# Loading b_re and b_im in their own order and turning them on TensorE, in a hybrid state space and attention layer

## The chip, the cores and the metric

The kernel runs on one core of a Trainium2 chip. The metric is the device time of one execution in microseconds (us), lower is better. A core has five engines with instruction queues of their own: TensorE (PE, matmuls and transposes, with PEld for its weight loads), VectorE (DVE), ScalarE (ACT), GpSimd (POOL) and SyncE (SP, which here only issues transfers). ACT can issue transfers too; in the profile such issues stand as ACTq, those of SP as SPq. Every engine works through its own queue in order, and semaphores order the engines among each other.

## The reference

One decoder layer on x of 512 tokens by 1024 channels, in float32. The part that the change touches is the state space branch: 64 groups of 16 channels, each with 64 complex states. From lambda, dt and B it makes a discrete system:

```
dt = exp(log_dt)[:, None]
ab = exp(lam_re * dt) * (cos(lam_im * dt) + i sin(lam_im * dt))     # [group, state]
f  = (ab - 1) / (lam_re + i lam_im)
bb_re = f_re[..., None] * b_re - f_im[..., None] * b_im              # [group, state, channel]
bb_im = f_re[..., None] * b_im + f_im[..., None] * b_re
```

u, a slice of `rms_norm(x) @ w_in`, is driven through `h[t] = ab * h[t-1] + bb u[t]`; the real part of C h plus a skip goes through GELU and a gated projection. The other branch is dilated attention with three head groups. Both are gated, added, projected and added to x. `b_re` and `b_im` have the shape (64 groups, 64 states, 16 channels): 256 KB each, 4 KB per group, and 64 bytes for one group and state.

## The kernel before, in words

All large matmuls are done three times on two-part operands (a rounded high part and a rest, `mm3`, L105 to L108). Weights come in tiles of 1024 x 128 or 512 x 256 through `load_w` (L160): a load into `w_raw` (two buffers) from the SP queue (L164), a high part on ACT (L91) and a rest on DVE, or for the first two tiles on POOL (L93), into `w_hi` and `w_lo` (three buffers). A raw buffer is free again when both parts have been made from it.

The start: four blocks of x are loaded (L191), with the first two weight tiles between them. For each half of x, ACT squares and sums (L206), DVE makes the reciprocal root (L98 to L103), ACT and DVE scale (L212, L214), PE transposes 16 blocks (L221) into four banks of PSUM, and ACT and DVE write the high part and the rest of hT from them (L225, L226). Then PE makes the first three tiles of u for each half (L282 to L287).

The coefficients: `lr`, `li` and `dt` (lambda and the log of dt) are loaded from the SP queue (L293 to L295). DVE works out exp, sine, cosine, f and the first eight powers `pw` of ab as [group, state] (L298 to L373). PE turns them to [state, group] (L383, L389), and ACT copies them to `AT` and `fT` (L385, L391). Positions (L477) and the weights of the head norms (L511, L513) are loaded from the SP queue too; DVE makes angles and tables from them.

B: `dd` is one tile with four parts of [128, 64 groups, 16 channels]: D1, D2, BB and BB2. D1 holds b_re in its lower 64 partitions (one per state) and b_im in the upper ones; D2 holds -b_im and b_re. Each of the four halves is a load from the SP queue through a view [state, group, channel] (L406 to L409), in runs of 16 floats, 64 bytes; POOL changes the sign of one half of D2 (L410). BB and BB2 are D1 and D2 times fT (L417 to L422, on POOL and DVE). They go into the coefficients `ab` of eight groups at a time (L248 to L250), which PE transposes (L267) for the states' inputs (L278); a scan over 64 chunks on DVE follows (L584, L588). Later D1 and D2 are used again as buffers for other matrices (L653). PSUM: `bank` (L83) hands out the four buffers with the tag "g", used by the transposes of x, by `atp`, `ftp` and by most steps after.

The order: the program is written in the order above, but the four loads of b stand behind the first tiles of u and the powers. A scheduler (L1030, `schedule_with_timeline_sim=True`) takes the instructions as a simulated timeline finds them ready, and writes the order of each engine's queue from that. So in the trace the loads of b are issued right behind those of x and lambda, well ahead of the place where the code has them. The orders of all queues are fixed before the run; a real wait then holds everything behind it on that queue.

Of the kernel before, what the change touches and what calls it, by code (L numbers as in the profile page):

```python
# [11 lines left out]
F32 = mybir.dt.float32  # L12
F32R = mybir.dt.float32r
I32 = mybir.dt.int32
AF = mybir.ActivationFunctionType
ALU = mybir.AluOpType
# [4 lines left out]
P = 128  # L21
# [3 lines left out]
NB = S // P  # L25
G = 64
N = 64
Q = 16
T = 8
C = S // T  # L30
# [20 lines left out]
def tile_hybrid_block(ctx: ExitStack, tc: tile.TileContext, x, positions, norm_w, w_in, lam_re, lam_im,  # L51
                      log_dt, b_re, b_im, c_re, c_im, d_skip, w_glu, q_norm_w, k_norm_w, w_ssm_out,
                      w_attn_out, w_o, out, dbg=None):
    nc = tc.nc
    pe, act, dve, pool, sp = nc.tensor, nc.scalar, nc.vector, nc.gpsimd, nc.sync
    dbg = dbg or {}

    cst = ctx.enter_context(tc.tile_pool(name="cst", bufs=1))
# [24 lines left out]
    def bank(name):  # L83
        return ps_g.tile([P, 512], F32, name=name, tag="g")
# [26 lines left out]
    n_ra = 2                          # residual gates of the attention branch done early  # L111
# [92 lines left out]
    for h in range(2):  # L204
# [10 lines left out]
        for q in range(KT // 2):  # L215
            ps = bank("hps")
# [23 lines left out]
    def coef(dst, j, a1, a2, n0, n1, t, eng):  # L240
        """dst[p, g, i, :] = re(A^(8-i)) a1 + im(A^(8-i)) a2, i in n0..n1, for the j-th run of groups"""
        n, ng = n1 - n0, dst.shape[1]
        sh = [P, ng, n, Q]
        gs = slice(ng * j, ng * j + ng)
        ar = AT[:, 0, gs, n0:n1].unsqueeze(3).broadcast_to(sh)
        ai = AT[:, 1, gs, n0:n1].unsqueeze(3).broadcast_to(sh)
        tv = t[:, 0:ng * n * Q].rearrange("p (g k q) -> p g k q", g=ng, k=n)
        dve.tensor_tensor(dst, a1.unsqueeze(2).broadcast_to(sh), ar, op=ALU.mult)  # L248
        eng.tensor_tensor(tv, a2.unsqueeze(2).broadcast_to(sh), ai, op=ALU.mult)  # L249
        dve.tensor_tensor(dst, dst, tv, op=ALU.add)  # L250
# [42 lines left out]
    sp.dma_start(lr, lam_re[0])  # L293
    sp.dma_start(li, lam_im[0])
    sp.dma_start(dt, log_dt.rearrange("o g -> g o"))  # L295

# [45 lines left out]
    # pw[:, 0/1, tau-1, :] powers 1..8 of the discrete diagonal; pw index 8 holds f  # L342
# [21 lines left out]
    for n in (1, 2, 4):  # L364
        # powers n+1..2n = (1..n) * n
        br_ = pw[:, 0:1, n - 1:n, :].broadcast_to([G, 2, n, N])
        bi_ = pw[:, 1:2, n - 1:n, :].broadcast_to([G, 2, n, N])
        a = pw[:, :, 0:n, :]
        o = pw[:, :, n:2 * n, :]
        dve.tensor_tensor(o, a, br_, op=ALU.mult)  # L370
        dve.tensor_tensor(tq[:, :, 0:n], a, bi_, op=ALU.mult)
        dve.tensor_tensor(o[:, 0], o[:, 0], tq[:, 1, 0:n], op=ALU.subtract)
        dve.tensor_tensor(o[:, 1], o[:, 1], tq[:, 0, 0:n], op=ALU.add)  # L373
    # to [state (twice), group]
    AT = cst.tile([P, 2, G, 9], F32, name="AT")         # powers 8 to 0
# [16 lines left out]
    # step of the chunk recurrence, [(parity, state), out, in, pair]  # L392
# [9 lines left out]
    # B: [re; im] and its rotation by i  # L402
    dd = big.tile([P, 4, G, Q], F32, name="dd", tag="s1")
    D1, D2, BB, BB2 = (dd[:, i] for i in range(4))
    bv = [b_re[0].rearrange("g n q -> n g q"), b_im[0].rearrange("g n q -> n g q")]
    sp.dma_start(D1[0:64], bv[0])  # L406
    sp.dma_start(D1[64:128], bv[1])
    sp.dma_start(D2[0:64], bv[1])
    sp.dma_start(D2[64:128], bv[0])  # L409
    pool.tensor_scalar(D2[0:64], D2[0:64], -1.0, None, op0=ALU.mult)  # L410
# [34 lines left out]
    def silu2(dst, ps):  # L445
        """2 silu"""
        th = t2k("th")
        act.activation(th, ps, AF.Tanh, scale=0.5)
        dve.scalar_tensor_tensor(dst, th, 1.0, ps, op0=ALU.add, op1=ALU.mult)  # L449
# [25 lines left out]
    # rope angles  # L475
# [33 lines left out]
    # weights of the head norms; q carries -1/8  # L509
# [17 lines left out]
    # tables: tC = [c w1, c w2], tS = [-s w2, s w1], per group, q/k, residue  # L527
# [12 lines left out]
    def tok_granule():  # L540
        """[token, 256] of two residues per bank"""
# [66 lines left out]
    gT_hi = big.tile([P, KT, S], F32R, name="gT_hi", tag="s3")  # L608
    gT_lo = big.tile([P, KT, S], F32R, name="gT_lo", tag="s4")
    kd = dram.tile([8, Q, 8, 240], F32, name="kd")      # lags 7..0, then 7 lags of zeros  # L610
# [4 lines left out]
    def ca_unit(j):  # L615
        """C A^k of groups 8j..8j+7"""
# [17 lines left out]
        # skip weights on the diagonal  # L634
# [5 lines left out]
    def m_unit(j, ca, dg):  # L640
        """the block Toeplitz matrices of groups 8j..8j+7"""
# [28 lines left out]
    def y_unit(j, ca, M, Uj, Ss):  # L670
        ysb = t2k("ysb").rearrange("c (t m) -> c t m", t=4)
        ps = bank("yps")
        for g in range(8):
            # the later half of a chunk comes first in M and ca, and goes to the upper partitions
# [9 lines left out]
    def g_unit(j, ysb):  # L684
# [3 lines left out]
        # [r h c] -> [r c h], then gelu  # L688
# [42 lines left out]
    def qk_granule(hp, g, QT, KA, KB):  # L731
# [16 lines left out]
        # rotary part of every head  # L748
# [30 lines left out]
    def scores(hp, QT, KA, KB):  # L779
        Pt = big.tile([P, 2, 2, NB, 256], F32, name="Pt", tag="s3")  # L780
        st = sml.tile([P, 2, 2, 2, NB], F32, name="st")      # kind (A, B), stat (-max, sum), head, block
# [33 lines left out]
        # put both orders together and weigh  # L815
# [219 lines left out]
```

## Time and profile before

| | us |
|---|---|
| median of 3 runs | 765.26 (764.66 to 765.6) |
| span of the profiled execution, first to last instruction | 761.9 |
| PE busy | 703.4 |
| DVE busy | 501.9 |
| ACT busy | 322.6 |
| POOL busy | 201.1 |

The profiled execution's own time is its span; what lies around it is the difference of 3.4 us to the median of the runs. A line of a timeline gives the start and the duration in us, engine, line of the code, operation, output and input, the count of instructions that were merged into it, and in brackets the engine's idle time just before and what ended it. A line of the waits gives the total, how often, and the longest. A line of a group gives the busy time, the mean of one in ns, and the idle time before. A line with two numbers and a colon is a stretch of time.

### The profile page before, as it was taken

Reading aid. Unit: us, or ns where it says so; the run is one execution under the profiler, and the core shown is the slowest. Engines: PE = TensorE matmul, PEld = TensorE weight load, DVE = VectorE, ACT = ScalarE, POOL = GpSimd, SP = SyncE. Lnnn points to the kernel's source line nnn. Section 1 sums busy time; section 2 is a strip of 40 time slices with the busy share of each in tenths; the row PEclk is TensorE's granted clock in tenths of the full one; section 3 lists DMA queues with packets and bytes.
Section 4 is the critical chain, followed back from the end, with each engine's and each line's share of the span. In section 5 each row is a group of like instructions: output and inputs, shape, how many; then the busy total and the mean of one; then the engine's idle time right before and its main releaser. Section 6 shows DMA issues by size and latency. Waiting matters only on the chain.

```text
span 761.9 us, 13588 instructions
## 1 busy us (share of the span) xinstructions
PE 703.4 (92%) x5221; PEld 616.4 (81%) x5221; DVE 501.9 (66%) x1239; ACT 322.6 (42%) x588; POOL 201.1 (26%) x318
## 2 busy tenths in 40 slices
PE   3698998896967969999999999999999999999998
PEld 2686886685846747888889999889989998878998
DVE  6767989999997643566334669757756764625631
ACT  6344442322435654433225447373446445523220
POOL 3456633433322100452001216224124131300000
PEclk9899999999888999999999999999999999999999
DMA  9755542552466576446433321312212321257331
GB/s 201 124 152 135 126 112 60 132 142 83 119 132 134 117 124 148 152 139 207 127 95 86 87 78 56 111 30 83 85 33 64 100 83 52 88 178 237 119 103 56
DMA packets 156016, 85.52 MB, mean 112 GB/s; under 512 B 40232, under 2 KB 148144, under 8 KB 155824
## 3 DMA queue, kind: packets, MB, share of 16 engines
q1 hardware_dynamic: 155936, 84.66, 42.4%
q8 instruction: 41, 0.67, 0.4%
q14 instruction: 23, 0.19, 0.1%
q10 hardware_dynamic: 16, 0.00, 0.0%
HBM read 73.18 MB, written 11.47 MB: 111 GB/s over the span
## 4 chain that ended last, share of the span: by engine, by line
PE 70%; DVE 17%; DMA 7%; SPq 3%; issue 2%; POOL 1%; ACT 0%; DVEq 0%; ACTq 0%
PE pj L108 19%; PE pj L107 19%; PE pj L106 19%; DVE Xs L588 6%; DVE ta L584 5%; DMA dd<-kd 4%; PE ot L866 2%; PE ptp L880 2%; PE sps L810 1%; PE qtp L767 1%; DMA Uj<-ud 1%; DVE ab L249 1%; DVE ab L248 1%; DVE ab L250 1%; PE yps L677 1%
## 5 line engine op out<-in xcount | busy, mean ns | idle before, releaser
L91 ACT ACTIVATE w_hi<-w_raw 128x1024 fp32r<-128x1024 f32 x100 | 105.8, 1059 | 187.8 <-PE pj L107 89.0
L106 PE MATMUL pj<-w_hi,hT_hi 128*128 128x256 f32 x512 | 144.7, 283 | 6.2 <-DVE z L449 6.2
L93 DVE TENSOR_TENSOR w_lo<-w_raw,w_hi 128x1024 fp32r<-128x1024 f32 x84 | 105.0, 1251 | 62.9 <-ACT w_hi L91 61.9
L107 PE MATMUL pj<-w_lo,hT_hi 128*128 128x256 f32 x512 | 144.6, 282 | 0.0
L108 PE MATMUL pj<-w_hi,hT_lo 128*128 128x256 f32 x512 | 144.4, 282 | 0.0
L106 PE MATMUL pj<-hT_hi,w_hi 128*128 128x512 f32 (+1 forms) x344 | 133.7, 391 | 7.3 <-ACT w_hi L91 5.8
L107 PE MATMUL pj<-hT_lo,w_hi 128*128 128x512 f32 (+1 forms) x344 | 133.1, 388 | 0.5 <-DVE hT_lo L226 0.5
L108 PE MATMUL pj<-hT_hi,w_lo 128*128 128x512 f32 (+1 forms) x344 | 133.0, 387 | 0.0
L106 PEld LDWEIGHTS pj<-w_hi,hT_hi 128*128 128x128 f32 x512 | 96.7, 189 | 7.4 <-DVE z L449 6.4
L107 PEld LDWEIGHTS pj<-w_lo,hT_hi 128*128 128x128 f32 x512 | 96.9, 189 | 1.4 <-issue 0.7
L108 PEld LDWEIGHTS pj<-w_hi,hT_lo 128*128 128x128 f32 x512 | 96.7, 189 | 0.7
L106 PEld LDWEIGHTS pj<-hT_hi,w_hi 128*128 128x128 f32 x344 | 65.9, 193 | 20.8 <-ACT w_hi L91 6.1
L108 PEld LDWEIGHTS pj<-hT_hi,w_lo 128*128 128x128 f32 x344 | 66.3, 193 | 14.0 <-issue 0.6
L107 PEld LDWEIGHTS pj<-hT_lo,w_hi 128*128 128x128 f32 x344 | 66.2, 192 | 14.0 <-DVE hT_lo L226 1.0
L588 DVE TENSOR_TENSOR Xs<-Xs,ta 128x32 f32<-128x32 f32 x252 | 56.4, 267 | 2.2
L93 POOL TENSOR_TENSOR w_lo<-w_raw,w_hi 128x1024 fp32r<-128x1024 f32 x16 | 41.0, 2564 | 49.3 <-ACT w_hi L91 38.4
L754 POOL TENSOR_TENSOR rt<-qraw,tC 128x256 f32<-128x256 f32 x12 | 16.8, 1397 | 126.7 <-DVE qraw L747 92.9
L584 DVE TENSOR_TENSOR ta<-Xs,A 128x64 f32<-128x64 f32 x126 | 43.3, 370 | 1.1
L107 PE MATMUL pj<-w_lo,mT_hi 128*128 128x256 f32 x128 | 36.2, 283 | 0.0
L108 PE MATMUL pj<-w_hi,mT_lo 128*128 128x256 f32 x128 | 36.2, 283 | 0.0
L106 PE MATMUL pj<-w_hi,mT_hi 128*128 128x256 f32 x128 | 36.2, 283 | 0.0
L739 DVE TENSOR_REDUCE ssq<-qsq 128x8 f32<-128x512 f32 x24 | 16.3, 684 | 26.1 <-ACT qsq L738 26.0
(252 smaller groups left out, 1370.7 us busy)
## 6 DMA issues: line engine op xcount, KB each, us to landing
w_raw<-in_w_in_dram SPq DMA_DIRECT2D x40, 512.0 KB
w_raw<-in_w_in_dram SPq DMA_DIRECT2D x64, 256.0 KB
Uj<-ud SPq DMA_DIRECT2D x16, 256.0 KB
dd<-kd SPq DMA_DIRECT2D x8, 512.0 KB
w_raw<-in_w_glu_dram SPq DMA_DIRECT2D x8, 512.0 KB
w_raw<-in_w_ssm_out_dram SPq DMA_DIRECT2D x8, 512.0 KB
w_raw<-in_w_o_dram SPq DMA_DIRECT2D x8, 512.0 KB
x_all<-in_x_dram SPq DMA_DIRECT2D x4, 512.0 KB
```

The source lines that it names most:

```text
L91: act.activation(hi, src, AF.Copy, scale=scale)
L93: e.tensor_tensor(lo, src, hi.bitcast(F32), op=ALU.subtract)
L106: pe.matmul(o, lh, rh, start=first, stop=False, skip_group_check=True)
L107: pe.matmul(o, lh, rl, start=False, stop=False, skip_group_check=True)
L108: pe.matmul(o, ll, rh, start=False, stop=last, skip_group_check=True)
L248: dve.tensor_tensor(dst, a1.unsqueeze(2).broadcast_to(sh), ar, op=ALU.mult)
L584: dve.tensor_tensor(ta[:, :, :, w], prev, A4[:, :, :, w], op=ALU.mult)
L588: dve.tensor_tensor(cur, cur, ta[:, :, i, w], op=ALU.add)
L739: dve.tensor_reduce(sq[:, 2 * b:2 * b + 2], s.rearrange("p (r h d) -> p r h d", r=2, h=4), AX.X, ALU.add)
L754: pool.tensor_tensor(t1, rh[:, :, :, 0:16], cv.broadcast_to([P, NB * 2, 2, 16]), op=ALU.mult)
L866: pe.matmul(o, v, pts[h][:, (2 * i + k) * P:(2 * i + k + 1) * P], start=first, stop=kind == 1 and b == NB - 1 and k == 1, skip_group_check ...
L880: pe.transpose(ps[:, (2 * i + k) * P:(2 * i + k + 1) * P], Pt[:, h, kind, 2 * bb + i, k * P:(k + 1) * P], ident)
```

## The change

`lr`, `li` and `dt` are loaded from the ACT queue. A new tile `bg` of [128, 64 states, 16 channels] takes b_re in its lower 64 partitions (one per group) and b_im in the upper ones, in two loads from the ACT queue with 4 KB in one run. PE turns it: for each of the 16 channels two matmuls with the identity write [state, (part, group)] to the lower and the upper half of a bank, four channels to a bank, so 32 in the program. ACT copies the parts from PSUM to D1 and D2 in 16 instructions of 64 partitions by 256 elements, one group of them with the factor -1. The four loads of D1 and D2 and the sign change on POOL are gone. `bg` uses the memory with the tag "s6b", which is free until then. The rest of the diff takes out comments.

```diff
-    sp.dma_start(lr, lam_re[0])
-    sp.dma_start(li, lam_im[0])
-    sp.dma_start(dt, log_dt.rearrange("o g -> g o"))
+    act.dma_start(lr, lam_re[0])
+    act.dma_start(li, lam_im[0])
+    act.dma_start(dt, log_dt.rearrange("o g -> g o"))
+    bg = big.tile([P, N, Q], F32, name="bg", tag="s6b")
+    act.dma_start(bg[0:G], b_re[0])
+    act.dma_start(bg[G:P], b_im[0])
...
     D1, D2, BB, BB2 = (dd[:, i] for i in range(4))
-    bv = [b_re[0].rearrange("g n q -> n g q"), b_im[0].rearrange("g n q -> n g q")]
-    sp.dma_start(D1[0:64], bv[0])
-    sp.dma_start(D1[64:128], bv[1])
-    sp.dma_start(D2[0:64], bv[1])
-    sp.dma_start(D2[64:128], bv[0])
-    pool.tensor_scalar(D2[0:64], D2[0:64], -1.0, None, op0=ALU.mult)
+
+    for q4 in range(4):
+        ps = bank("btp")
+        pv = ps.rearrange("p (q a g) -> p q a g", q=4, a=2)
+        for q in range(4):
+            for h in range(2):
+                pe.matmul(ps[64 * h:64 * h + 64, q * P:(q + 1) * P], bg[:, :, 4 * q4 + q], ident, start=True, stop=True,
+                          skip_group_check=True)
+        qs = slice(4 * q4, 4 * q4 + 4)
+        for h in range(2):
+            sl = slice(64 * h, 64 * h + 64)
+            act.copy(D1[sl, :, qs], pv[sl, :, h].rearrange("p q g -> p g q"))
+            if h == 0:
+                act.activation(D2[sl, :, qs], pv[sl, :, 1].rearrange("p q g -> p g q"), AF.Copy, scale=-1.0)
+            else:
+                act.copy(D2[sl, :, qs], pv[sl, :, 0].rearrange("p q g -> p g q"))
```

## The prediction

> **What bounds the kernel now.** I read the page first, then the chain of waits over the first 50 us, then the SP queue, the waits and each engine's timeline in that stretch.
>
> ```profile
> span 761.9 us, 13588 instructions
> ...
> DMA packets 156016, 85.52 MB, mean 112 GB/s; under 512 B 40232, under 2 KB 148144, under 8 KB 155824
> ...
> PE 70%; DVE 17%; DMA 7%; SPq 3%; issue 2%; POOL 1%; ACT 0%; DVEq 0%; ACTq 0%
> ```
>
> TensorE carries 70% of the chain, VectorE 17%, both without a break from about 45 us on. So work moved off another engine is worth nothing as such; what counts is how early the long PE stretch gets going, and whether the change puts new PE work into it. The 3% of SPq is odd for a queue that only issues transfers. Its timeline shows where it lies:
>
> ```profile
> 8.41 0.65 SPq L406 DMA_DIRECT2D dd<-in_b_re_dram  x1
> 9.10 5.12 SPq L407 DMA_DIRECT2D dd<-in_b_im_dram  x1
> 14.26 2.54 SPq L408 DMA_DIRECT2D dd<-in_b_im_dram  x1
> 16.84 2.81 SPq L409 DMA_DIRECT2D dd<-in_b_re_dram  x1
> 19.70 3.70 SPq L477 DMA_DIRECT2D scr<-in_positions_dram  x1
> 23.44 0.43 SPq L511 DMA_DIRECT2D scr<-in_q_norm_w_dram  x1
> ...
> 24.47 0.38 SPq L164 DMA_DIRECT2D w_raw<-in_w_in_dram  x1
> ```
>
> The four loads of b hold SP from 8.41 to 19.65, and the positions load behind them takes 3.70 us to issue where its neighbours take 0.43: the queue is full of short packets. (Four loads of 256 KB in 64-byte runs are 16,384 packets, two fifths of the 40,232 short ones of the page.) The third weight load, L164, comes only at 24.47. The next fence is the list of waits between 20 and 32 us (total, times, longest), then the PE timeline.
>
> ```profile
> ACT w_hi L91 <- DMA w_raw<-in_w_in_dram: 7.3, 1, 7.3
> ...
> DVE scr L479 <- DMA scr<-in_positions_dram: 2.6, 1, 2.6
> ...
> DVE w_lo L93 <- ACT w_hi L91: 1.7, 1, 1.7
> ...
> DVE scr L515 <- DMA scr<-in_q_norm_w_dram: 0.7, 1, 0.7
> ```
>
> ```profile
> 12.90 3.68 PE L221 MATMUL hps<-ident,x_all 128*128 128x128 f32 x16 [10.41 <-DVE x_all L214]
> ...
> 23.54 1.91 PE L221 MATMUL hps<-ident,x_all 128*128 128x128 f32 x16
> 31.29 0.58 PE L106 MATMUL pj<-hT_hi,w_hi 128*128 128x256 f32 x1 [5.84 <-ACT w_hi L91]
> ```
>
> PE finishes the second set of transposes of x at 25.45 and then stands for 5.84 us until the third weight tile is split. In stretches of that part (length, PE busy and count, granted clock, DMA share, GB/s):
>
> ```profile
> 31.29:35.27 3.98, 3.94 (x16) 0.50 0.48 137
> 35.27:44.38 9.11, 9.11 (x81) 1.00 0.05 14
> ```
>
> After the wait PE ran 3.98 us at half clock. At full clock those matmuls take half of that, so the wait cost 5.84 + 1.99 = 7.83 us.
>
> **What the change removes.** With the four b loads gone, SP issues positions after log_dt, at about 8.4, and the two norm weights, at 0.43 to 0.65 each: free by about 10. The third weight load also needs its raw buffer, the one of the first weight tile, whose split ends on POOL at 9.30 + 2.35 = 11.65:
>
> ```profile
> 9.30 2.35 POOL L93 TENSOR_TENSOR w_lo<-w_raw,w_hi 128x1024 fp32r<-128x1024 f32 x1 [7.17 <-ACT w_hi L91]
> ...
> 30.18 1.06 ACT L91 ACTIVATE w_hi<-w_raw 128x1024 fp32r<-128x1024 f32 x1 [7.34 <-DMA w_raw<-in_w_in_dram]
> ```
>
> It took 30.18 - 24.47 = 5.7 us from issue to use, with the rest of b still draining; from 11.7 that gives 17.4 at the latest. ACT in its present order reaches this split at 22.84 (the L212 row below), so it waits for nothing: w_hi is done at 23.9, w_lo 1.23 later at 25.1, before PE ends its transposes at 25.45. The 5.84 us and the cold stretch both go: -7.83. The three loads of lambda and dt also leave SP, but SP then waits for the buffer anyway: nothing. POOL's sign flip of D2 goes too; POOL waited for DVE behind it, so it gives nothing either.
>
> **What it adds.** Five issues on the ACT queue, two DMAs that now run beside those of x, 32 written matmuls on PE, and 16 copies on ACT that fill D1 and D2.
>
> ```profile
> 0.73 0.58 ACTq L181 DMA_DIRECT2D nw<-in_norm_w_dram  x1
> ...
> 5.07 1.06 ACT L206 ACTIVATE junk<-x_all 128x1024 f32<-128x1024 f32 x1 [2.43 <-DMA x_all<-in_x_dram]
> ...
> 12.09 1.15 ACT L212 ACTIVATE x_all<-x_all,scr 128x1024 f32<-128x1024 f32 x1 [1.39 <-DVE scr L103]
> ...
> 17.34 1.57 ACT L225 ACTIVATE hT_hi<-hps,nwc 128x256 fp32r<-128x256 f32 x4 [0.67 <-DVE hT_lo L226]
> 19.32 0.48 ACT L225 ACTIVATE hT_hi<-hps,nwc 128x256 fp32r<-128x256 f32 x1 [0.41 <-DVE hT_lo L226]
> 21.69 1.15 ACT L212 ACTIVATE x_all<-x_all,scr 128x1024 f32<-128x1024 f32 x1 [1.89 <-DVE scr L103]
> ```
>
> Issues: 5 x 0.58 = 2.9 us ahead of the first Square, which had 2.43 us of idle time: +0.5, and everything on ACT behind it (both Squares, then the chain to the first transposes) shifts by that.
>
> DMAs: the two loads are 512 KB in 4 KB rows, issued near 4 us, while x and the first weights stream:
>
> ```profile
> 5.00:12.00 7.00, 1.00 1.12 334
> 12.00:23.00 11.00, 1.00 1.20 91
> ```
>
> (Clock, DMA share, GB/s: full rate for x and weights, a quarter of it while b drains in 64-byte runs.) At 334 GB/s 0.524 MB are 1.6 us of a saturated system. The cost lies between 0, if they are served behind x on whatever is free, and 1.6, if all of it comes ahead of the second block of x. I take 0.8, the middle, since the issue falls halfway through the first two blocks' transfers. The Trainium skill, "DMA: Bandwidth & Descriptors", section "Queues, rings and completion order", speaks against the move to a second queue: each DMA engine takes turns packet by packet between the queues that have work, so a load on ACT's queue is not served behind SP's. No row of before shows two loaded queues. By it alone the term is the 1.6 and my sum would be 0.8 higher, 761.0; by a queue that serves in order it would be 759.4.
>
> PE: 32 written, but the trace counts twice as many for the like step L383 (2 x 8 x 2 = 32 in the code), so 64. The nearest shape, f32 with 128 moving columns, is L646, eight of them between 131.51 and the next at 131.86:
>
> ```profile
> L383 PE MATMUL atp<-ident,pw x64: 218/218/267, 44.5 to 51.8; 64*64 64x64 f32 x64
> ```
>
> ```profile
> 131.51 0.41 PE L646 MATMUL kps<-ab,dd 128*16 128x128 f32 x8 [1.65 <-DVE ab L250]
> 131.86 0.44 PE L625 MATMUL cps<-ident,cn 128*128 128x128 f32 x2
> ```
>
> That is 0.044 us each, 2.8 us in all at full clock, 5.6 at half. The scheduler's order decides where they fall. b is issued by 0.73 + 6 x 0.58 = 4.2 and, with half the bytes of the weight load that took 5.7, lands near 9 (an estimate), while PE stands until 12.90 (row above). Most likely they run there, ending at 14.6 if all are cold: 1.7 late, but the first 16 transposes, which took 3.68 against 1.91 for the second set, then run warm and give 1.77 back: 0. The bound above is 2.8, in the full stretch after 45 us; the one below is a rival of its own.
>
> ACT copies: 64 partitions x 256 elements out of PSUM, read with a stride. By the rows of the first 56 us (busy, mean ns):
>
> ```profile
> L225 ACT ACTIVATE hT_hi<-hps,nwc 128x256 fp32r<-128x256 f32 x16 | 6.5, 470 | 1.2 <-DVE hT_lo L226 1.1
> L256 ACT COPY uT<-pj 128x512 f32<-128x512 f32 x4 | 4.3, 1116 | 0.0
> ...
> L385 ACT COPY AT<-atp 128x512 f32<-128x512 f32 x2 | 1.1, 592 | 0.6 <-PE atp L383 0.6
> ```
>
> Same size, L225: in a run 1.57 / 4 = 0.39 apart, so 16 are 6.3 us. Ends: half of L385, 0.30 each, 4.7 us, and half of L256, 0.56 each, 8.9 us. I take 6.3, by the row of the same length. Between 10.7 and 21.7 ACT has idle pieces of 1.39 + 0.67 + 0.41 + 1.89 = 4.36 us; those hide part, and 1.9 us come ahead of hT_hi, on the path: +1.9 (0 to 8.9). BB needs D1 first at 52.92, when it waits for fT, so late copies hurt no reader.
>
> Next late when PE moves up: the powers pw on DVE. PE's atp matmuls stood close behind them:
>
> ```profile
> 43.33 0.28 DVE L373 TENSOR_TENSOR pw<-pw,tq 64x128 f32<-64x128 f32 x1
> ...
> 44.47 1.20 PE L383 MATMUL atp<-ident,pw 64*64 64x64 f32 x32
> ```
>
> A margin of 0.86. DVE's waits for positions, norm weights and the split (2.6 + 0.7 + 1.7 = 5.0) go as well, so DVE allows PE 5.9 us. My front gain is -7.83 + 0.5 + 0.8 + 1.9 = -4.6, inside that: 0 more.
>
> **Sum.** 761.9 - 4.6 = 757.3 us of span. The runs' median, 765.26, is 3.4 above the profiled span; that part lies outside the first and last instruction and stays: 760.7.
>
> **The rivals.**
>
> *Warm front.* The turning ends before 12.90, the copies fit into idle time, and DMAs cost nothing. The 1.77 us of the first transposes are then a clear gain. The VectorE chain before them also had one 2.23 us instruction, on two elements per partition, while POOL split the first weight:
>
> ```profile
> 9.43 2.23 DVE L101 TENSOR_TENSOR scr<-scr 128x2 f32<-128x2 f32 x1
> ```
>
> If that falls away, 2.1 go too. PE would gain 7.83 + 1.77 + 2.1 = 11.7, but DVE allows 5.9 + 2.1 = 8.0: 757.3; 753.6 if atp is ordered later. For it: PE's empty 10.4 us. Against it: ACT's idle time is short. The Trainium skill, "TensorE: Matmul & The Clock Gate", part 1, says full clock comes after about 3.4 us of busy time and is lost after an idle window of the same length. By that the gain needs turning work that ends just before the transposes; the half-clock stretch of 3.98 us after 5.84 idle agrees, the gain itself no row shows.
>
> *Slower: the turning stands ahead of x.* The queues are in order and the turning uses the four "g" banks that the transposes of x need. If all four are given to it first, the first transposes wait for b to land (9), a quarter of the matmuls cold (1.4), and up to 16 copies at 0.39 to 0.56 (6.3 to 8.9) mixed with ACT's own Square, split and scale (1.06 + 1.06 + 1.15 = 3.3): 20.0 to 22.6 instead of 12.90. That is 7.1 to 9.7 late; from 7.8 on the whole gain is eaten, and at the upper end the kernel is 1.9 slower: 767.2. For it: b is ready before the scaled x. Against it: x comes first in the program.
>
> *No change.* The whole order is planned anew, so SP may put the third weight load behind another waiting transfer, or a later wait may take the gain back: 765. PE's longest later waits (total, times, longest) are of that size:
>
> ```profile
> PE yps L677 <- DMA Uj<-ud: 9.0, 2, 4.5
> PE pj L106 <- DVE z L449: 7.7, 2, 6.2
> ```
>
> For it: both sit where a transfer or VectorE, not PE, comes last. Against it: VectorE and the transfers there start from results of the same front.
>
> **How the numbers follow.** 0.2%, 1.5 us, is about what can be told from no change. Forecast with its own bounds (757.5 to 763.7): 0.52. Warm front: 0.18. No change: 0.14. Slower: 0.16. Faster 0.70, same 0.14, slower 0.16. The range reaches from 754.0, near the warm front's end, to 766.5, most of the way to the slower rival, leaving some 0.2 outside.
>
> **What would show it.** Right: no b load on SP, L164's third issue near 12, no PE wait on w_hi near 25 us, clock full from 16 us on, b's copies on ACT before 30 us, the atp matmuls near 40. Wrong: the first transposes of x after 13.5, hT_hi behind D1 copies on ACT, a PE wait on pw, or the front early and the scan no earlier.

## The result, and the profile after

The changed kernel takes 771.79 us (median of 4 runs, 770.99 to 774.44) against 765.43 for the kernel before beside it (4 runs): a ratio of 1.0084, 95% interval 1.0062 to 1.0106. That is 6.4 us slower, where 4.6 faster was forecast, and outside the range. The profiled span went from 761.9 to 769.3; the changed kernel's profiled run took 771.06, so 1.8 us lie outside its span where 3.4 were reckoned for the kernel before, and up to 1.6 of the 7.4 may come of that. The page of the changed kernel, its span, packets and chain:

```profile
span 769.3 us, 13735 instructions
...
DMA packets 139728, 85.00 MB, mean 110 GB/s; under 512 B 23816, under 2 KB 131728, under 8 KB 139536
...
PE 67%; DVE 17%; DMA 10%; issue 2%; ACT 2%; SPq 1%; POOL 0%; DVEq 0%; ACTq 0%
```

The change did what it says: 40,232 - 23,816 = 16,416 short packets are gone, and SPq fell from 3% of the chain to 1%. (From here on, lines behind L295 have moved by 3, and by 13 behind the turning.) SP's timeline of the changed kernel:

```profile
6.42 0.33 SPq L191 DMA_DIRECT2D x_all<-in_x_dram  x1
8.33 0.33 SPq L490 DMA_DIRECT2D scr<-in_positions_dram  x1
...
14.55 0.33 SPq L633 DMA_DIRECT2D cn<-in_c_im_dram  x1
...
16.79 0.38 SPq L164 DMA_DIRECT2D w_raw<-in_w_in_dram  x1
```

Positions issues in 0.33 us instead of 3.70, and the third weight load comes at 16.79 instead of 24.47. It does not come at 11.7, because SP now stands elsewhere; these are the longest waits of its queue up to 20 us (total, times, longest):

```profile
SPq L633 <- DMA w_raw<-in_w_in_dram: 3.1, 1, 3.1
SPq L191 <- DMA x_all<-in_x_dram: 2.8, 1, 2.8
```

Still, PE's wait of 5.84 for the third weight split is gone. What took its place stands in the waits of the changed kernel between 10 and 33 us and in VectorE's timeline:

```profile
PE pj L107 <- DVE hT_lo L226: 2.0, 1, 2.0
PE pj L108 <- DVE w_lo L93: 1.2, 1, 1.2
```

```profile
7.94 0.22 DVE L354 TENSOR_TENSOR scr<-scr 64x64 f32<-64x64 f32 x1 [1.10 <-DMA scr<-in_lam_im_dram]
...
11.12 0.15 DVE L307 TENSOR_SCALAR scr<-scr 64x1 f32<-64x1 f32 x1 [1.90 <-DMA scr<-in_log_dt_dram]
...
13.64 0.75 DVE L214 TENSOR_SCALAR x_all<-x_all,scr 128x1024 f32<-128x1024 f32 x1
```

VectorE works in order. Lambda is planned earlier now, so its first steps were put in front of and into the reciprocal root chain of x (L98 to L103), and there VectorE waits for their transfers. The scaling of x, L214, starts at 13.64 instead of 12.09, and the first transposes at 14.45 instead of 12.90. PE then runs at half clock for long, as its timeline shows:

```profile
14.45 1.97 PE L221 MATMUL hps<-ident,x_all 128*128 128x128 f32 x8 [11.29 <-DVE scr L317]
...
24.35 0.58 PE L108 MATMUL pj<-hT_hi,w_lo 128*128 128x256 f32 x1 [1.17 <-DVE w_lo L93]
...
30.37 0.39 PE L108 MATMUL pj<-hT_hi,w_lo 128*128 128x256 f32 x1
30.59 0.29 PE L106 MATMUL pj<-hT_hi,w_hi 128*128 128x256 f32 x1
30.72 0.28 PE L107 MATMUL pj<-hT_lo,w_hi 128*128 128x256 f32 x1
```

The starts lie 0.21 to 0.22 apart up to 30.59, and 0.11 to 0.13 after. So the front gained nothing: PE's atp begins at 44.89 (44.47 before). Then comes the loss. The timelines of PE, ACT and VectorE from there:

```profile
44.89 2.08 PE L386 MATMUL atp<-ident,pw 64*64 64x64 f32 x64
...
47.14 1.19 PE L414 MATMUL btp<-ident,bg 128*64 128x128 f32 x16
...
51.97 3.18 PE L414 MATMUL btp<-ident,bg 128*64 128x128 f32 x48 [2.51 <-ACT AT L388]
```

```profile
50.38 1.06 ACT L91 ACTIVATE w_hi<-w_raw 128x1024 fp32r<-128x1024 f32 x1 [4.31 <-DMA w_raw<-in_w_in_dram]
51.34 1.06 ACT L388 COPY AT<-atp 128x512 f32<-128x512 f32 x2
52.29 0.28 ACT L394 COPY fT<-ftp 128x128 f32<-128x128 f32 x1
52.44 0.37 ACT L419 COPY dd<-btp 64x256 f32<-64x256 f32 x1
...
57.32 0.37 ACT L423 COPY dd<-btp 64x256 f32<-64x256 f32 x1
```

```profile
57.45 1.22 DVE L431 TENSOR_TENSOR dd<-dd,fT 128x1024 f32<-128x1024 f32 x1 [4.75 <-ACT dd L419]
```

The same place in the kernel before, ACT and VectorE:

```profile
50.02 1.06 ACT L91 ACTIVATE w_hi<-w_raw 128x1024 fp32r<-128x1024 f32 x1 [4.26 <-DMA w_raw<-in_w_in_dram]
51.65 1.08 ACT L385 COPY AT<-atp 128x512 f32<-128x512 f32 x2 [0.57 <-PE atp L383]
```

```profile
52.92 1.23 DVE L418 TENSOR_TENSOR dd<-dd,fT 128x1024 f32<-128x1024 f32 x1 [0.58 <-ACT fT L391]
```

Read them together. The turning (btp) did not go into the hole of the start; it stands behind atp, in the full stretch, with 1.19 + 3.18 = 4.37 us of PE and a wait of 2.51 for banks. The banks are held because ACT, in order, stands 4.31 in front of a weight split (L91) whose raw tile has not landed. Behind that split are queued AT, fT and the 16 copies. BB starts at 57.45 instead of 52.92, and waits 4.75 for the copies. Before, AT and fT stood behind the same split, and AT then waited 0.57 more for the second half of atp, which PE had only at 50.82 to 52.06.

What PE makes of it stands at the first transposes of the coefficients (wps) and the first states' inputs (xps), before and then after:

```profile
69.95 1.09 PE L267 MATMUL wps<-ident,ab 128*128 128x128 f32 x8 [1.08 <-DVE ab L250]
74.15 1.09 PE L267 MATMUL wps<-ident,ab 128*128 128x128 f32 x8 [1.47 <-DVE ab L250]
81.01 1.20 PE L278 MATMUL xps<-Uj,W 128*64 128x64 f32 x32
```

```profile
72.00 1.06 PE L267 MATMUL wps<-ident,ab 128*128 128x128 f32 x8 [0.80 <-DVE ab L250]
86.72 1.17 PE L278 MATMUL xps<-Uj,W 128*64 128x64 f32 x32 [0.63 <-DMA Uj<-ud]
```

From atp to the first xps PE takes 41.8 us instead of 36.5. Of these 5.3 the matmuls of the turning hold PE for 4.2, and the waits add 1.4 (2.51 + 0.80 + 0.63, against 1.08 + 1.47). The late BB shows as a wait of only 0.80 for ab, since the turning and the wait for banks have held PE back about as long. The path through BB and PE's own work are late by much the same, so taking away one of them need not bring back the whole (e2 and e3, below).

Most of the loss is there early: xps begins at 86.7 instead of 81.0, 5.7 late, and the scan, 108.6 instead of 102.9, is as late. The rest of the 7.4 comes by the last yps at 307.3 instead of 299.9. PE's waits there are no longer in all; but from the first yps to the last it is busy for 80.1 instead of 77.3 us on 840 matmuls, at a granted clock of 0.91 instead of 0.93. From there to the end nothing changes.

### The profile page after: what moved, and what is told of

Read it like the earlier page. It is cut to its first block, busy times and chain, and to the rows that moved or that the text cites. A ratio compares the mean times of both kernels' runs of the same rounds, so it can differ in the third digit from the quotient of the medians.

```text
span 769.3 us, 13735 instructions
## 1 busy us (share of the span) xinstructions
PE 711.9 (93%) x5285; PEld 625.0 (81%) x5285; DVE 497.0 (65%) x1239; ACT 328.0 (43%) x604; POOL 199.0 (26%) x317
## 2 busy tenths in 40 slices
DMA packets 139728, 85.00 MB, mean 110 GB/s; under 512 B 23816, under 2 KB 131728, under 8 KB 139536
## 4 chain that ended last, share of the span: by engine, by line
PE 67%; DVE 17%; DMA 10%; issue 2%; ACT 2%; SPq 1%; POOL 0%; DVEq 0%; ACTq 0%
PE pj L108 18%; PE pj L107 18%; PE pj L106 18%; DVE Xs L601 6%; DVE ta L597 4%; DMA dd<-kd 4%; DMA Uj<-ud 4%; PE ot L879 2%; PE ptp L893 2%; DMA w_raw<-in_w_in_dram 2%; PE sps L823 1%; PE qtp L780 1%; DVE ab L249 1%; DVE ab L250 1%; DVE ab L248 1%
## 5 line engine op out<-in xcount | busy, mean ns | idle before, releaser
L91 ACT ACTIVATE w_hi<-w_raw 128x1024 fp32r<-128x1024 f32 x100 | 105.9, 1060 | 192.0 <-PE pj L107 95.7
L93 DVE TENSOR_TENSOR w_lo<-w_raw,w_hi 128x1024 fp32r<-128x1024 f32 x84 | 107.8, 1284 | 68.0 <-ACT w_hi L91 67.1
L107 PE MATMUL pj<-hT_lo,w_hi 128*128 128x512 f32 (+1 forms) x344 | 134.9, 393 | 2.0 <-DVE hT_lo L226 2.0
L106 PE MATMUL pj<-hT_hi,w_hi 128*128 128x512 f32 (+1 forms) x344 | 135.4, 395 | 1.3 <-DVE z L462 1.3
L108 PE MATMUL pj<-hT_hi,w_lo 128*128 128x512 f32 (+1 forms) x344 | 134.6, 392 | 1.2 <-DVE w_lo L93 1.2
L106 PEld LDWEIGHTS pj<-hT_hi,w_hi 128*128 128x128 f32 x344 | 67.6, 197 | 14.7 <-DVE z L462 1.7
L601 DVE TENSOR_TENSOR Xs<-Xs,ta 128x32 f32<-128x32 f32 x252 | 56.4, 267 | 2.2
L597 DVE TENSOR_TENSOR ta<-Xs,A 128x64 f32<-128x64 f32 x126 | 40.3, 347 | 1.1
```

The lines of the kernel that those rows point to most:

```text
L91: act.activation(hi, src, AF.Copy, scale=scale)
L93: e.tensor_tensor(lo, src, hi.bitcast(F32), op=ALU.subtract)
L106: pe.matmul(o, lh, rh, start=first, stop=False, skip_group_check=True)
L107: pe.matmul(o, lh, rl, start=False, stop=False, skip_group_check=True)
L108: pe.matmul(o, ll, rh, start=False, stop=last, skip_group_check=True)
L597: dve.tensor_tensor(ta[:, :, :, w], prev, A4[:, :, :, w], op=ALU.mult)
```

## The experiments

The theory: the turning costs little by itself, but ACT's order puts its copies behind a weight split that waits for a transfer, and they hold BB; the loads on ACT's queue cost something of their own. The rivals: the matmuls and copies are the price wherever they stand; the second queue alone is it. Ratios are to the kernel before on the same chip, with 95% intervals; the next column is the ratio less 1, times 765.5 us. First starts (hps are the transposes of x, wps those of the coefficients) are from one profile of each; those of e4, e5, e6 and m8 are of the longest of their runs.

| kernel | ratio | us to before | first hps | BB | first wps |
|---|---|---|---|---|---|
| before | | 0 | 12.9 | 52.9 | 70.0 |
| as changed | 1.0084 (1.0062 to 1.0106) | +6.4 | 14.4 | 57.4 | 72.0 |
| e1_no_b | 0.9946 (0.9925 to 0.9967) | -4.1 | 12.7 | 43.0 | 62.0 |
| e10_sp_no_turn | 0.9944 (0.9922 to 0.9966) | -4.3 | 12.9 | 43.5 | 62.6 |
| e9_sp_no_copies | 0.9949 (0.9924 to 0.9974) | -3.9 | 13.0 | 41.8 | 63.6 |
| e5_b_sp | 1.0074 (1.0059 to 1.0089) | +5.7 | 13.0 | 57.0 | 71.5 |
| e7_e1_b_act | 0.9968 (0.9952 to 0.9984) | -2.4 | 11.5 | 44.9 | 63.8 |
| e8_e1_lam_act | 1.0036 (1.0023 to 1.0049) | +2.8 | 15.8 | 52.5 | 68.0 |
| e2_no_turn | 1.0040 (1.0023 to 1.0057) | +3.1 | 14.3 | 52.6 | 69.2 |
| e3_no_copies | 1.0073 (1.0052 to 1.0093) | +5.6 | 14.5 | 52.5 | 72.4 |
| e4_lam_sp | 1.0108 (1.0087 to 1.0130) | +8.3 | 11.0 | 59.3 | 73.8 |
| e6_b_late | 1.0041 (1.0025 to 1.0058) | +3.1 | 12.7 | 56.4 | 70.9 |
| m1_coef_first_sp | 0.9998 (0.9979 to 1.0017) | -0.2 | 13.0 | 49.0 | 64.7 |
| f3_early_sp_o | 0.9994 (0.9978 to 1.0010) | -0.5 | 12.8 | 48.7 | 64.1 |
| m5_coef_first_before | 1.0034 (1.0017 to 1.0051) | +2.6 | 12.7 | 52.4 | 68.3 |
| m6_early_coef_first_sp | 0.9938 (0.9916 to 0.9959) | -4.7 | 13.0 | 41.0 | 61.5 |
| m7_mended_all_act | 0.9982 (0.9966 to 0.9998) | -1.4 | 14.6 | 41.4 | 64.5 |
| m8_mended_b_act | 0.9985 (0.9969 to 1.0001) | -1.1 | 13.1 | 49.4 | 66.6 |

**What the four loads cost.** e1_no_b is the kernel before without them; D1 and D2 are filled with a constant, so B is left out.

```diff
-    sp.dma_start(D1[0:64], bv[0])
...
-    pool.tensor_scalar(D2[0:64], D2[0:64], -1.0, None, op0=ALU.mult)
+    pool.memset(D1, 0.25)
+    pool.memset(D2, 0.25)
```

> The kernel before without its four loads of b: GpSimd fills D1 and D2 with a constant instead, so B is left out. By the theory of the prediction (the loads hold the SP queue, the third weight tile comes late, PE stands 5.84 us and then runs cold) about 757.5 us, 7.8 less than before, and the 144 first matmuls end near 36.5 us instead of 44.4. By the theory formed from the trace after (with the loads gone the planner puts other waits into the front: positions ahead of hT on VectorE, PE at half clock between short gaps) the front ends at 42 to 45 us all the same, and the time is 763 to 766 us.

It gains 4.1 (2.5 to 5.7), about halfway between the two expectations. PE's wait for the third split shrinks from 5.84 to 0.5, but new ones for VectorE, 2.1 in all, take part of its place. BB starts ten microseconds earlier than before, since AT and fT are now planned ahead of the waiting split; so the gain is not that of the shorter wait alone.

**The loads in long runs, on SP.** e10_sp_no_turn has lambda and b, 4 KB in a run, all on SP, without matmuls and copies (B left out as in e1).

```diff
+    sp.dma_start(bg[0:G], b_re[0])
+    sp.dma_start(bg[G:P], b_im[0])
...
+    pool.memset(D1, 0.25)
+    pool.memset(D2, 0.25)
```

> All five loads on SP in 4 KB runs, without the turning: no matmuls and no copies, D1 and D2 are filled with a constant by POOL, so the output leaves B out. Theory 1 (loads in long runs on SP cost nearly nothing, the matmuls in the stretch after 40 us some 1 to 2): 760 to 761.5, like the kernel without any load of B (760.9). Rival (the loads themselves push x and the weights by some 3, as they did on the ACT queue): 763 to 764, and the matmuls then cost nothing.

-4.3 against -4.1: the two long loads on SP cost nothing that can be measured, as theory 1 had it.

**Queue.** e7_e1_b_act is e1 with the two loads of b on ACT, unread; e8_e1_lam_act is e1 with lambda and dt on ACT. Both leave B out.

```diff
+    act.dma_start(bg[0:G], b_re[0])
+    act.dma_start(bg[G:P], b_im[0])
```

```diff
-    sp.dma_start(lr, lam_re[0])
...
+    act.dma_start(lr, lam_re[0])
...
```

> The first experiment (no loads into D1 and D2, GpSimd fills them with a constant, B left out) plus the two loads of b on the ACT queue, which nobody reads; lambda and dt on SP. It parts the 8 us between that experiment and the changed kernel without the turning. If b beside x is the cost, 767 to 771 us. If the moved lambda and dt are, 760 to 762 us.

> The first experiment (D1 and D2 filled with a constant, B left out) with lambda and dt on the ACT queue instead, and no load of b: the other half of the 8 us. If b beside x is the cost, 760 to 762.5 us. If the moved lambda and dt are, with the new orders that the planner makes from it, 766 to 769 us.

e7 lies between its two expectations. With b beside x, 2.4 of the gain of 4.1 are left; the intervals touch, so the 1.7 between them is not settled by these two alone (m8, below, has it again). The place is ACT's first weight split, in e1 and then in e7:

```profile
7.95 1.06 ACT L91 ACTIVATE w_hi<-w_raw 128x1024 fp32r<-128x1024 f32 x1 [0.52 <-DMA w_raw<-in_w_in_dram]
```

```profile
11.54 1.06 ACT L91 ACTIVATE w_hi<-w_raw 128x1024 fp32r<-128x1024 f32 x1 [3.22 <-DMA w_raw<-in_w_in_dram]
```

The first weight tile comes 3.6 us later, and PE waits 2.2 for a split instead of 0.5. That is more than the 1.6 that the prediction reckoned for b's bytes from the rate of 334 GB/s. The rule of the Trainium skill, "DMA: Bandwidth & Descriptors", section "Queues, rings and completion order", that an engine takes turns packet by packet between queues, points this way, and the trace agrees in direction; the delay of the tile was beyond the upper bound that I had set for the cost.

Lambda on ACT, 32 KB and a few bytes, costs 6.9 (from -4.1 to +2.8), more than the 512 KB of b. VectorE's timeline in e8 shows lambda's steps amid the root chain of x, and ACT's the rest:

```profile
8.26 0.22 DVE L351 TENSOR_TENSOR scr<-scr 64x64 f32<-64x64 f32 x1 [0.47 <-DMA scr<-in_lam_im_dram]
...
14.94 0.75 DVE L214 TENSOR_SCALAR x_all<-x_all,scr 128x1024 f32<-128x1024 f32 x1
```

```profile
45.26 0.63 ACT L385 COPY AT<-atp 128x512 f32<-128x512 f32 x1
50.30 1.06 ACT L91 ACTIVATE w_hi<-w_raw 128x1024 fp32r<-128x1024 f32 x1 [4.42 <-DMA w_raw<-in_w_in_dram]
51.27 0.57 ACT L385 COPY AT<-atp 128x512 f32<-128x512 f32 x1
```

The front is late by 3.1 (15.8 against 12.7). Most of that is one more small instruction that lasted 2.3 us instead of 0.16 (e1 has one such in this chain, e8 two; last section); the rest is the wait of 0.47 for lambda, and its steps. And the new plan puts one half of AT behind the waiting split: BB 52.5. So this price, too, is largely one of order.

**The turning in its place.** e2_no_turn has the changed kernel's five loads on ACT but neither matmuls nor copies; e3_no_copies has the matmuls and no copies. D1 and D2 are constants in both.

```diff
-    for q4 in range(4):
-        ps = bank("btp")
...
+    pool.memset(D1, 0.25)
+    pool.memset(D2, 0.25)
```

```diff
-            act.copy(D1[sl, :, qs], pv[sl, :, h].rearrange("p q g -> p g q"))
...
+    pool.memset(D1, 0.25)
```

> The changed kernel with its two loads of b, but without the 64 matmuls and the 16 copies: GpSimd fills D1 and D2 with a constant, so B is left out. If the turning is what makes the change slower (4.4 us of matmuls in PE's full stretch, 2.5 us of PE waiting for a bank, or the copies ahead of BB), 764 to 766 us, as before. If the loads on the ACT queue or the new order of the front make it slower, 769 to 772 us.

> The changed kernel with the loads and the 64 matmuls, but without the 16 copies: GpSimd fills D1 and D2 with a constant, so B is left out. If the matmuls on PE cost the time (4.4 us of work, and up to 2.5 us of wait for a bank), 768.5 to 771 us. If the copies do (VectorE waited 4.75 us for them before BB), 765 to 767 us.

Half of the loss, +3.1, is there without any turning; the matmuls bring it to +5.6, the copies to +6.4, within the interval of the step before. e2 thus lies between its expectations, and e3 with the one that blames the matmuls. Taken alone, this would clear the copies. But in these two kernels AT and fT stand behind the waiting split anyway, so BB comes at 52.5, as before and not at 41 to 43 as in the faster kernels, with or without copies.

That e2 is slower than the kernel before with the same BB is a matter of order again. Its order has the first wps 72 matmuls of pj (the projections) behind atp, where the kernel before has 92. PE comes there early and waits for ab in one piece:

```profile
69.16 1.97 PE L267 MATMUL wps<-ident,ab 128*128 128x128 f32 x8 [5.12 <-DVE ab L250]
```

After that wait it runs at a granted clock of 0.50 (70.7 to 74), and the next 24 matmuls take 7.8 us, against 5.9 in the changed kernel. The first xps, at 85.9, is 4.9 late.

**One queue or the other.** e4_lam_sp takes lambda and dt back to SP; e6_b_late besides gives bg the memory of another buffer, which is free only after x has been squared, so that b comes later; e5_b_sp has all five loads on SP. Nothing is left out in these.

```diff
-    act.dma_start(lr, lam_re[0])
+    sp.dma_start(lr, lam_re[0])
...
```

```diff
-    bg = big.tile([P, N, Q], F32, name="bg", tag="s6b")
+    bg = big.tile([P, N, Q], F32, name="bg", tag="s6a")
```

```diff
-    act.dma_start(bg[0:G], b_re[0])
-    act.dma_start(bg[G:P], b_im[0])
+    sp.dma_start(bg[0:G], b_re[0])
+    sp.dma_start(bg[G:P], b_im[0])
```

> The changed kernel with the loads of lambda and dt back on the SP queue; b stays on the ACT queue. If the late lambda and dt on VectorE (1.1 and 1.9 us of waits inside the root of the first half of x, first transposes at 14.45 us instead of 12.90) pass through to the end, 768.5 to 770 us. If the front has slack for them, since half-clock PE work and later waits follow, 770.5 to 772.5 us like the changed kernel.

> The changed kernel with all five moved loads back on the SP queue, b still in 4 KB runs: b is then issued behind x and the first two weight tiles. If b on a second queue beside x and the weights is what costs the front (second weight tile at 14.6 us instead of 13.2, ACT and VectorE waiting, PE at half clock), the front ends near 41 us as without b, the turning still costs its 3 us, and the time is 762.5 to 765.5 us. If the loads cost it by their bytes wherever they are issued, 769 to 772 us.

> The changed kernel with lambda and dt on SP, and b on the ACT queue in the memory of the Square's scrap tile (tag s6a), so that both loads can start only after the last Square, behind x. If it is the time at which b's 512 KB flow that costs the front, 762.5 to 766 us. If issues of transfers on the ACT queue cost it, now between the copies of hT, 769 to 773 us.

None comes out below the kernel before, so the queue alone is not the cause: with everything on SP, and a front that is 3.6 us earlier than before (first atp 40.9 against 44.5), the change still costs 5.7. e4 is slower than both its expectations: its first transposes are 3.4 earlier than in the changed kernel, but lambda on SP brings another order, in which AT and fT come early and twelve copies stand behind a split that waits 5.98. e6 comes out just below its second expectation. ACT in e5, and what PE waits for in e5 between 45 and 105 us:

```profile
43.34 1.08 ACT L388 COPY AT<-atp 128x512 f32<-128x512 f32 x2 [0.40 <-PE atp L386]
44.91 0.37 ACT L419 COPY dd<-btp 64x256 f32<-64x256 f32 x1 [0.48 <-PE btp L414]
...
52.21 1.06 ACT L91 ACTIVATE w_hi<-w_raw 128x1024 fp32r<-128x1024 f32 x1 [6.01 <-DMA w_raw<-in_w_in_dram]
...
56.86 0.37 ACT L423 COPY dd<-btp 64x256 f32<-64x256 f32 x1
```

```profile
PE wps L267 <- DVE ab L250: 6.9, 1, 6.9
```

Four copies are done by 46; the other twelve stand behind the split, which waits 6.01. BB starts at 57.0, ab is late, and PE, in order, waits 6.9 at the first wps.

**The copies alone.** e9_sp_no_copies is e5 with its 64 matmuls but without copies (D1 and D2 constant, B left out).

```diff
-            act.copy(D1[sl, :, qs], pv[sl, :, h].rearrange("p q g -> p g q"))
...
+    pool.memset(D1, 0.25)
+    pool.memset(D2, 0.25)
```

> The change with all five loads on SP in 4 KB runs, and the 64 matmuls of the turning, but without the 16 ACT copies (D1 and D2 are filled with a constant by POOL, so the output leaves B out). Theory 1 (the copies delay BB, and with it ab and the whole long stretch): BB starts near 44 instead of 57, the long PE stretch pays only for the matmuls, about 3 to 4 us: 764 to 766, 6 to 8 below the version with copies (772.4). Rival (the copies sit in ACT idle time and harm no reader, the matmuls and the loads are the price): 770 to 772.

+5.7 becomes -3.9: the 16 copies, 0.33 apart and 5.3 us of ACT, cost 9.6 us of the kernel's time in this order, and the 64 matmuls beside the loads 0.4, within the interval (e9 against e10). This is theory 1, and lower than it gave: the 3 to 4 us that it set down for the matmuls do not show in the time. They are in the trace, though, at 41.2 to 46.7: e9's atp begins 1.5 earlier than e10's, and e10 waits 1.5 for ab, which e9 does not. VectorE in e9:

```profile
41.84 1.23 DVE L425 TENSOR_TENSOR dd<-dd,fT 128x1024 f32<-128x1024 f32 x1 [0.59 <-ACT fT L394]
```

**Mending the order.** m1_coef_first_sp and f3_early_sp_o are e5 with one part of the program moved; m5_coef_first_before is the same move as in m1 on the kernel before.

```diff
-    first = [(get_w(), ps_p.tile([P, 512], F32, name="pj", tag="pj")) for _ in range(3)]
...
-        u_unit(j, first[j][1])
     lr = scr([G, N])
...
+    first = [(get_w(), ps_p.tile([P, 512], F32, name="pj", tag="pj")) for _ in range(3)]
...
+        u_unit(j, first[j][1])
     sgn = cst.tile([P, 1], F32
```

```diff
+    for q4 in range(4):
+        ps = ps_o.tile([P, 512], F32, name="btp", tag="o")
...
     def exp_exact(dst, src, shape, pfx):
...
-    for q4 in range(4):
-        ps = bank("btp")
```

> The change with all five loads on SP, and in the program the first three tiles of u stand behind the code of BB, so that the coefficients and the turning come first in the scheduler's order. Nothing is left out. Theory 1 (what costs is that AT, fT and the 16 copies stand on ACT behind weight splits that wait for a transfer): BB starts 47 to 50, the matmuls of the turning fall among the early ones with holes, 763 to 767. Rival (the matmuls and copies cost what they cost wherever they stand): 770 to 773, as with the old order (772.4).

> The change with all five loads on SP, with the turning written in the program ahead of the exponentials and with another PSUM bank than the transposes of x use, so that its matmuls lie in the early holes of PE; AT and fT stay where they are, behind a weight split on ACT. Nothing is left out. Theory 1 (AT and fT behind the split decide with the copies): the matmuls cost 0 instead of 3 to 4, the copies come earlier, BB at 51 to 53, still late for ab: 766 to 769. Rival (only the matmuls in the full stretch cost): 762 to 764. Second rival (early copies on ACT delay hT_hi and with it the front): 772 or more.

> Control: the kernel before (four loads in 64-byte runs on SP, no turning) with the first three tiles of u moved behind the code of BB in the program. Theory 1: before, BB waits only for fT at 52.9 and the PE wait at 31.29 for the third weight tile stays, so the new place gives little: 763 to 766. Rival (the new place is a gain by itself, whatever is done with B): 758 to 761, as much as it gives the changed kernel.

m1 and f3 each take some 6 us off e5, to no measurable difference from before. In m1 VectorE still waits 5.0 for the copies, since 48 of the matmuls stand on PE behind the second half of atp, at 44.05 (BB 49.0; that the "g" banks made the scheduler put them there is argued); in f3 most copies are early, but AT and fT stand behind the split (BB 48.7, earlier than the 51 to 53 expected, and the time lies between theory 1 and its first rival). m5 makes the kernel before 2.6 slower, more than theory 1 gave it: the move is no gain by itself. It helps because it brings B.

m6_early_coef_first_sp has both of these moves, on e5:

```diff
+        ps = ps_o.tile([P, 512], F32, name="btp", tag="o")
...
+        u_unit(j, first[j][1])
     sgn = cst.tile([P, 1], F32
```

> Both mends together: all five loads on SP, the turning written ahead of the exponentials and with a PSUM bank that the transposes of x do not use, and the first three tiles of u behind the code of BB in the program. Nothing is left out. Theory 1 (the time hangs on when BB can start, through ab and the first transposes of the coefficients): BB at 42 to 45, first wps 62 to 64, 760 to 763, below both kernels. Rival (the 64 matmuls and 16 copies have a price wherever they stand): 764 to 766, as each mend alone.

0.9938 (0.9916 to 0.9959), 4.7 us faster than before and 11 faster than the change as written: the fastest of all with B in it, level with the kernels that have none. PE in m6:

```profile
12.97 3.68 PE L221 MATMUL hps<-ident,x_all 128*128 128x128 f32 x16 [10.49 <-DVE x_all L214]
16.57 1.98 PE L301 MATMUL btp<-ident,bg 128*64 128x128 f32 x16
...
18.85 0.28 PE L107 MATMUL pj<-hT_lo,w_hi 128*128 128x256 f32 x1
18.97 0.28 PE L108 MATMUL pj<-hT_hi,w_lo 128*128 128x256 f32 x1
```

A quarter of the turning fills the hole behind the first transposes, and PE goes on at 0.11 to 0.12 a matmul from 18.85, at the full rate twelve microseconds before the kernel as changed. All copies are done by 36.9, ACT has fT at 40.63, and PE has no wait for ab.

**Queue again, with the order mended.** m7_mended_all_act is m6 with all five loads on ACT, as the change has them; m8_mended_b_act has only b there.

```diff
-    sp.dma_start(lr, lam_re[0])
+    act.dma_start(lr, lam_re[0])
...
-    sp.dma_start(bg[0:G], b_re[0])
-    sp.dma_start(bg[G:P], b_im[0])
+    act.dma_start(bg[0:G], b_re[0])
+    act.dma_start(bg[G:P], b_im[0])
```

> The change with its five loads on ACT as written, and the two mends of the order (turning early in another PSUM bank, first tiles of u behind the code of BB). Nothing is left out. Theory 1 (lambda on the ACT queue costs by itself: VectorE gets lambda's work planned into the reciprocal root chain of x and waits there for the transfer, so the first transposes of x start at 14 to 16 instead of 13.0, and PE then has waits and half clock): 763.5 to 767. Rival (the queue matters only through the order, which is mended here): 760 to 761.5, as with SP.

> The same mended order, lambda and dt on SP, only the two loads of b on ACT. Nothing is left out. Theory 1 (b beside x is harmless once the order is right, lambda is what costs): 760 to 762, first transposes near 13. Rival (b on a second queue takes turns with x and the weights, 1.6 us of traffic): 762.5 to 764, first transposes of x or the first weight split later by 1 to 2.

Both give back most of m6's 4.7 (3.3 and 3.6, each known to about 2). m7 has the time and the signs of theory 1: first transposes 14.6, lambda's waits of 1.24 and 1.29 again before and within the root chain. But m8, with lambda on SP, is as slow, so m7 does not show that lambda is what costs; no run has lambda alone on ACT in the mended order. m8 (764.4 by its ratio) is nearer to its rival, and 0.4 above it: b on the second queue is not harmless. Only the start of m8 is read here, PE and ACT:

```profile
11.16 1.98 PE L301 MATMUL btp<-ident,bg 128*64 128x128 f32 x16 [8.67 <-DMA bg<-in_b_im_dram]
```

```profile
11.81 1.06 ACT L91 ACTIVATE w_hi<-w_raw 128x1024 fp32r<-128x1024 f32 x1 [4.20 <-DMA w_raw<-in_w_in_dram]
```

The first weight split comes at 11.81, against 8.23 in m6. Here a quarter of the turning stands ahead of x, and is over just when the first transposes of x begin (13.1).

## Why the prediction was wrong

By the trace, the forecast was missed in two places. It had atp near 40 and nothing new behind it; atp came at 44.89, 5 us later, and from there to the first xps PE took 5.3 more than before. By the runs, the loss splits into three parts: m6 against before -4.7, ACT's queue in place of SP's +3.3 (m7 less m6), the order as the scheduler made it +7.8 (as changed less m7). The last two are differences that are known to about 2 us; the sum, +6.4, is that of the result by construction. The parts depend on each other: in the unmended order the queue seems to cost 0.7 only (as changed less e5); that the late BB hides the rest is argued.

- **What the four b loads hold: sized too high, mechanism right.** SP was held by them, the wait of 5.84 vanished, short packets fell by about the number forecast. But -7.83 came out as -4.1 (e1): I took "the cold stretch" as gone along with the wait. New waits (1.79 and 0.52 in e1, 2.00 and 1.17 in the changed kernel) were followed by a half rate up to 25.66 in e1 and up to 30.59 in the changed kernel. L164 came at 16.79 and not near 12, behind other loads that waited on SP.
- **Issues, +0.5: nothing.** The first Square begins at 5.10 against 5.07. Only two of the five issues stand ahead of it; that of dt comes at 5.11, and dt is what VectorE then waits 1.90 for.
- **"The three loads of lambda and dt also leave SP ... nothing": failed.** I looked at the queue that they leave, not at the engine that reads them. An early load made the scheduler place its readers early, in VectorE's chain for x, where they wait. e8 put 6.9 on it, with the order that came of it. It hangs on that order: m7 and m8, with and without lambda on ACT, differ by 0.3.
- **DMAs beside x, 0.8 (0 to 1.6): too small.** The first weight split is 3.6 later in e7 and in m8, and m8 less m6 is +3.6 in time. In the changed kernel, where b is issued at 5.61 and 6.62, it is the second weight tile that is late: ACT waits 3.67 for it and splits it at 14.56 instead of 13.15, with the scaling of x behind it.
- **Turning on PE, "Most likely they run there ... 0": failed for the kernel as changed.** It ran behind atp, at 47 to 55, for 4.37, with 2.51 of wait for banks between. My bound for that case, 2.8, was low as well: 64 in 4.37 is 0.068 each, not 0.044. Where an order allowed it (m6), no cost shows.
- **"so late copies hurt no reader": failed, and with it the reading of BB.** The size was right, 0.33 apart against 0.39, and none came ahead of hT_hi, so the 1.9 that the sum set down there was not paid. But fT, at 52.61 before, was itself late: it stood on ACT behind a split without data, and behind PE's late second half of atp. I read "BB waits for fT" as slack for the copies. In the changed kernel they are queued behind the same split and behind fT, and BB waits 4.75 for them. e9 puts 9.6 us on the copies in e5's order; in the changed kernel, where the turning holds PE about as long, taking out the copies alone gives 0.8, within the interval (e3). What decided is the order that puts all that BB needs behind that split, and the turning into the full stretch: mended, it gives 7.8 (m7).
- **"that part ... stays", 3.4 outside the span: failed by 1.6.** It was the span of one execution against the median of others; in the changed kernel's profiled run it is 1.8. With 1.8 the sum would have come out 1.6 lower, further off. Beside it, 761.0 and 759.4 are slips: 760.7 plus and minus 0.8 is 761.5 and 759.9.
- **Rivals.** The slower rival had the sign, but not the size (1.9 at its upper end against 6.4) nor the place: the turning stands behind atp. m8 has a quarter of the turning ahead of x, in another PSUM bank, and its first transposes are not late. "No change" named a new order that puts the third weight load behind a waiting transfer, or a later wait that takes the gain back; the first is part of what happened, and the later wait came at BB and not at Uj or z. The warm front did not come as told (the first 16 transposes take 3.68 in m6 too), but in m6 PE is at the full rate from 18.85 on.
- **Left open.** Why the scheduler places the first wps after 72 matmuls of pj in e2 and after 92 in the kernel before. m6 and m7 mend two places of the order at once, and the share of each in the 7.8 is not shown with the loads on ACT. Lambda alone on ACT was not run in the mended order.

## What to carry to other kernels

A step that is cheap on a partly idle engine is priced by what it is queued behind, not by its length: look for the in-order neighbour that waits for a transfer, and for the reader behind both. In a kernel whose order is planned by a scheduler, each load that is moved also moves its readers; compare the orders of the engines before trusting a sum of durations. A removal that shows a part to cost nothing (the copies, in e3) is to be repeated where the wait beside it is gone.

## What the runs showed of the hardware that was not expected

VectorE's smallest instructions can take 2.2 us: one on two elements per partition, 0.16 elsewhere, lasted until a split on POOL ended. In e8 it happened twice in one chain, VectorE's rows and POOL's:

```profile
9.37 2.20 DVE L103 SCALAR_TENSOR_TENSOR scr<-scr 128x2 f32<-128x2 f32 x1
...
12.40 2.31 DVE L102 SCALAR_TENSOR_TENSOR scr<-scr 128x2 f32<-128x2 f32 x1
```

```profile
9.21 2.34 POOL L93 TENSOR_TENSOR w_lo<-w_raw,w_hi 128x1024 fp32r<-128x1024 f32 x1 [5.24 <-ACT w_hi L91]
12.36 2.34 POOL L93 TENSOR_TENSOR w_lo<-w_raw,w_hi 128x1024 fp32r<-128x1024 f32 x1 [0.81 <-ACT w_hi L91]
```

9.37 + 2.20 = 11.57 and 9.21 + 2.34 = 11.55; 14.71 and 14.70. That VectorE is held by POOL is argued from these ends, and was not tried by itself.

PE took long to warm: in the kernel as changed its last pause ended at 24.35, and the full rate came at 30.59, 6.2 us later; in e1 it was 6.1 us, from 19.59 to 25.66. The Trainium skill, "TensorE: Matmul & The Clock Gate", part 1, gives about 3.4 us of busy time and warns that its window is free-running; both are longer than the 3.4, and within two such windows, 6.8 by an estimate from the page's figure. The granted clock of the changed kernel's stretch from 24.35 to 30.59 is given as 1.00, so the half rate there is read from the spacing of the matmuls; in e1 it is 0.50.

An issue can stand for an earlier load that it does not depend on: with lambda and b on ACT, SP's L633 (a load of C) stood 3.1 for a weight load, and the fourth load of x, issued at 6.42, stood 2.8 for an earlier load of x. That this comes of the second queue is not shown. With everything on SP such waits are there too, if shorter (1.3 at L616 and at L617 in e1, 1.6 at L526 in m6), and before, where the fourth load of x did not wait, its issue lasted from 3.47 to 6.49. Why the loads are tied was not tried.
